# A decoder layer in which the low halves of the RWKV weights and the log decays move from GpSimd to VectorE

## The chip, the core and the metric

The kernel runs on one core of a Trainium2 chip. A core has five engines that run their own instruction queues in order and wait for each other by semaphores: TensorE (PE; its weight loads are listed as PEld), VectorE (DVE), ScalarE (ACT), GpSimd (POOL) and SyncE (SP), which here only issues DMAs. The metric is the device time of one execution in microseconds (us), lower is better. About 0.2% (3.2 us) is what a measurement of this kernel can tell from no change.

## What is computed

One layer with two branches that share an input projection and an output projection; the norms and the attention are left out here.

```python
xn = rms_norm(h, norm_w)
p = jnp.einsum('bsd,dn->bsn', xn, w_in)            # 1024 x 1024 by 1024 x 8320, fp32
p_tm = p[..., :SHIFT_COLS]                          # r, k, v, decay rank, iclr rank
p_tm = p_tm + (prev - p_tm) * mu_shift              # token shift
y_rwkv = rwkv7_time_mix(p_tm, p[..., RWKV_GATE0:ATT0], ...)
y_att = mixed_dilated_attention(p[..., ATT0:ATT_GATE0], p[..., ATT_GATE0:])
h = h + jnp.einsum('bsm,md->bsd', jnp.concatenate([y_rwkv, y_att], -1), w_out)

# in rwkv7_time_mix, for 16 heads of 64:
w = -jax.nn.softplus(-(w0 + jnp.tanh(w_lo) @ w_up)) - 0.5
decay = jnp.exp(-jnp.exp(w))                        # log decay = -exp(-0.5) * sigmoid(...)
state = (state * w_t[:, :, None, :] + sa[..., None] * bv_t[:, :, None, :]
         + v_t[..., None] * k_t[:, :, None, :])     # one step of the recurrence
```

## The kernel before

**Projections.** A product of fp32 precision is made of three products of fp32r parts: x is split into a high part `xh` and a low part `xl`, and each block of 128 columns of `w_in` into `wh` and `wl`. `wload` (L169) brings one such block in two halves of 128 x 512 (`wraw`, two buffers), ScalarE rounds a half to `wh` (L178), and GpSimd subtracts it from the raw half to make `wl` (L179). `wh` and `wl` have two buffers each, so a block can be split as soon as TensorE has done the last product with the block before the last. `stream` (L190) is a generator that loads one block ahead and yields after each of the 24 products of a block and a half of the tokens (`pq`, L187).

**The RWKV stage.** There are 16 units: 8 pairs of heads times 2 halves of 512 tokens; unit n is half n mod 2 of pair n // 2, so odd units are second halves. A unit runs a chain of 8 chunks of 64 tokens, each of three steps (`chain`, L636): `z` from the state (`Sd`), copied to `zd` by VectorE and ScalarE (L654, L655); `z` from `zd` and the inverse `U`, scaled to `ud` (L657, L658); and `T` from `ud` and `TU`, scaled to the next `Sd` (L657, L658). TensorE must wait for both halves of each copy. While one unit's chain runs, the next unit's matrices are prepared, those of the one after are begun, and the finished one is normed. `rwkv` (L287) puts all this into 24 slots a unit and fills TensorE with four projections a slot, 96 a unit.

**Decays.** In `prepare`, `decay` (L400) computes `th` by ScalarE (L408); GpSimd makes the log decays `lw` (L413) in a tile that shares its memory with `W`, after a memset of its last column (L412); VectorE sums them backwards in four scans (`I`, L422), and ScalarE's exponentials of `I` (`W`, `Ux`) scale `AR` and `BK`, from which TensorE makes `pa` (L527). VectorE masks one half of `pa` into `TU` (L530), ScalarE copies the other into `MV` (L533), and GpSimd masks that (L534).

**Order.** The order on an engine is not that of the code. A scheduler places every instruction when, by its own estimate of durations, its inputs are ready, and prefers what stands earlier in the code. A change of engine in one line thus moves other instructions too, on all engines.

After the RWKV stage come the attention, which takes its projections from the same stream (columns from `ATT0` on), and the output projection.

Of the kernel before, what the change touches and what calls it, by code (L numbers as in the profile page):

```python
# [9 lines left out]
F32 = mybir.dt.float32  # L10
# [3 lines left out]
ALU = mybir.AluOpType  # L14
# [10 lines left out]
C = 64  # L25
NC_ = HALF // C
LO0 = 3072
GATE0 = 3200
ATT0 = 4224
# [15 lines left out]
DECAY = float(np.exp(-0.5))  # L45
# [4 lines left out]
def bc(ap, shape):  # L50
    return ap.broadcast_to(list(shape))


class Kern:
# [111 lines left out]
                V.tensor_tensor(out=self.xl[h][:, 4 * b:4 * b + 4, ts], in0=q, in1=hi.bitcast(F32), op=ALU.subtract)  # L166
                yield

    def wload(self, src, wp):  # L169

        nc = self.nc
        wl = wp.tile([128, KT, 128], F32R, name="wl")
        wh = wp.tile([128, KT, 128], F32R, name="wh")
        for i in range(2):
            raw = wp.tile([128, KT // 2, 128], F32, name="wraw")
            ks = slice(4 * i, 4 * i + 4)
            nc.sync.dma_start(out=raw, in_=src[i * 512:(i + 1) * 512].rearrange("(kt p) c -> p kt c", p=128))
            nc.scalar.copy(out=wh[:, ks], in_=raw)  # L178
            nc.gpsimd.tensor_tensor(out=wl[:, ks], in0=raw, in1=wh[:, ks].bitcast(F32), op=ALU.subtract)  # L179
        return wh, wl  # L180

    def proj_steps(self, w, h, q):
# [6 lines left out]

    def stream(self, jobs):  # L190

        load = lambda job: self.wload(self.t["w_in"][:, job[0]:job[0] + 128], self.wp)
        w = load(jobs[0])
        for i, (_, halves, take) in enumerate(jobs):
            wn = load(jobs[i + 1]) if i + 1 < len(jobs) else None
            for h in halves:
                q = self.ps_proj.tile([128, HALF], F32, name="pq", tag="proj")
                steps = self.proj_steps(w, h, q)
                for m in steps[:-1]:
                    m()  # L200
                    yield
                steps[-1]()
                take(h, q)
                yield
            w = wn
# [85 lines left out]
    def rwkv(self, pairs=range(NPAIR), apairs=range(NPAIR)):  # L291
        nc = self.nc
        with ExitStack() as ctx:
# [21 lines left out]
            for a in self.ARs:  # L315
                nc.gpsimd.memset(a[:, NC_ * 192:], 0.0)
                a = self.c192(a)
                for e in range(2):
                    er = slice(e * 64, e * 64 + 64)
                    nc.gpsimd.tensor_copy(out=a[er, :, 0], in_=bc(self.ident[er, er].unsqueeze(1), (64, NC_, 64)))  # L320
            self.d0 = pers.tile([128, 2, C + 1], F32, name="d0")
            nc.gpsimd.memset(self.d0, 1.0)
            nc.gpsimd.memset(self.d0[:, :, C:C + 1], 0.0)
            bank = lambda p, tag: lambda: p.tile([128, 4, 128], F32, name="xq", tag=tag)
# [66 lines left out]
    def prepare(self, d):  # L391

        nc = self.nc
        V, S, G = nc.vector, nc.scalar, nc.gpsimd
        h, pr = d["h"], d["pr"]
        col = lambda base: self.prm[:, base + pr:base + pr + 1]
        c3 = lambda ap: ap.rearrange("p (c t) -> p c t", t=C)
        L = (128, NC_, C + 1)

        def decay():  # L400
            zq = self.ps_a.tile([128, HALF], F32, name="zq", tag="pa0")
            aq = self.ps_a.tile([128, HALF], F32, name="aq", tag="pa1")
            hi, lo = d["lw"]
            for i, q in enumerate((zq, aq)):
                nc.tensor.matmul(q, lhsT=hi[i], rhs=self.lx[h][i], start=True, stop=False)
                nc.tensor.matmul(q, lhsT=lo[i], rhs=self.lx[h][i], start=False, stop=True)
            th = self.tmp("gt0", "th")
            S.activation(out=th, in_=zq, func=AF.Tanh, scale=0.5, bias=self.hw0[:, pr:pr + 1])  # L408
            ta = d["ta"] = self.tmp("gt1", "ta")
            S.activation(out=ta, in_=aq, func=AF.Tanh, scale=0.5, bias=self.ha0[:, pr:pr + 1])  # L410
            lw = self.tmp("vr0", "lw", L)
            G.memset(lw[:, :, C:C + 1], 0.0)  # L412
            G.tensor_scalar(out=lw[:, :, 0:C], in0=c3(th), scalar1=-DECAY / 2, scalar2=-DECAY / 2,  # L413
                            op0=ALU.mult, op1=ALU.add)
            d["lw_"], d["I"] = lw, self.tmp("gt0", "I", L)

        def sums(i):

            for c in (4 * i, 4 * i + 2):
                fl = lambda a, c=c: a[:, c:c + 2].rearrange("p c t -> p (c t)")[:, ::-1]  # L420
                z0 = fl(self.d0, 0)
                V.tensor_tensor_scan(out=fl(d["I"]), data0=z0, data1=fl(d["lw_"]), initial=0.0, op0=ALU.mult,  # L422
                                     op1=ALU.add)
            if i == 0:
                return
            I = d["I"]
            W = d["W"] = self.tmp("vr0", "W", L)
            S.activation(out=W, in_=I, func=AF.Exp, scale=-1.0)
            Ux = d["Ux"] = self.tmp("vr1", "Ux", L)
            S.activation(out=Ux, in_=I, func=AF.Exp)  # L430
            d["dec"] = self.mid.tile([64, 2, NC_], F32, name="dec", bufs=3)
            G.tensor_copy(out=d["dec"][:, 0], in_=Ux[0:64, :, 0])
            S.copy(out=d["dec"][:, 1], in_=Ux[64:128, :, 0])

        def norm():
            sq = self.tmp("qr1", "sq")
            S.activation(out=sq, in_=d["ks"], func=AF.Square, scale=col(P_KK))
            sqt = self.ps_tr.tile([128, 4, 2, HD], F32, name="sqt", tag="tr")
            for b in range(4):
                nc.tensor.transpose(out=sqt[:, b].rearrange("p a b -> p (a b)"), in_=sq[:, b * 128:(b + 1) * 128],  # L440
                                    identity=self.ident)
            nq = self.mid.tile([128, 4, 2], F32, name="nq")
            V.tensor_reduce(out=nq, in_=sqt, axis=AX.X, op=ALU.add)
            rn = d["rn"] = self.mid.tile([128, NC_], F32, name="rn", bufs=3)
            for par in range(2):
                for e in range(2):
                    V.tensor_scalar(out=rn[e * 64:e * 64 + 64, par::2], in0=nq[par * 64:par * 64 + 64, :, e], scalar1=1e-24,
                                    scalar2=-2.0, op0=ALU.max, op1=ALU.mult)
            V.reciprocal(out=rn, in_=rn)
            d["rn1"] = self.mid.tile([64, NC_], F32, name="rn1", bufs=3)  # L450
            S.copy(out=d["rn1"], in_=rn[64:128])

        def removal():
            ks, ta, W, Ux = d["ks"], d["ta"], d["W"], d["Ux"]
            BK = d["BK"] = self.lng.tile([128, NC_, 128], F32, name="BK", bufs=1)
            V.scalar_tensor_tensor(out=self.c192(d["AR"])[:, :, 2], in0=c3(ks), scalar=col(P_KK), in1=W[:, :, 0:C],
                                   op0=ALU.mult, op1=ALU.mult)
            b2 = BK[:, :, 0:64]
            V.scalar_tensor_tensor(out=b2, in0=c3(ta), scalar=1.0, in1=Ux[:, :, 1:C + 1], op0=ALU.add, op1=ALU.mult)
            V.scalar_tensor_tensor(out=b2, in0=c3(ks), scalar=col(P_KK), in1=b2, op0=ALU.mult, op1=ALU.mult)  # L460
            S.activation(out=ta, in_=ta, func=AF.Identity, scale=self.hka[:, pr:pr + 1], bias=self.oka[:, pr:pr + 1])
            V.tensor_tensor(out=ks, in0=ks, in1=ta, op=ALU.mult)
            V.tensor_tensor(out=BK[:, :, 64:128], in0=c3(ks), in1=Ux[:, :, 1:C + 1], op=ALU.mult)

        def receptance():
            V.tensor_tensor(out=self.c192(d["AR"])[:, :, 1], in0=c3(d["rs"]), in1=d["W"][:, :, 1:C + 1], op=ALU.mult)

        def bonus_parts():
            rs = d["rs"]
            V.scalar_tensor_tensor(out=rs, in0=rs, scalar=self.hrk[:, pr:pr + 1], in1=d["ks"], op0=ALU.mult, op1=ALU.mult)  # L470
            bh, bl = d["bs"] = [self.tmp(t, n, dt=F32R) for t, n in (("kr3", "bh"), ("vr3", "bl"))]
            S.copy(out=bh, in_=rs)
            G.tensor_tensor(out=bl, in0=rs, in1=bh.bitcast(F32), op=ALU.subtract)
        return list(zip(PREP, (norm, decay, lambda: sums(0), lambda: sums(1), removal, receptance, bonus_parts)))

    def late(self, d):
# [623 lines left out]
```

## Time and profile before

| | us |
|---|---|
| median of 3 runs (1586.15 to 1588.06) | 1586.47 |
| the profiled execution | 1586.58 |
| its span, from the first to the last instruction | 1584.9 |
| PE busy | 1492.5 |
| DVE busy | 1014.7 |
| ACT busy | 892.7 |
| POOL busy | 532.9 |

The span and the execution's time differ by 1.7 us, which lie outside the instructions. The profile is read here in four views: the page's sums and its chain of work that ended last; stretches of time with the busy time of each engine; the timeline, with each instruction's start and duration and the idle time of its engine before it; and groups of instructions by line. The busy time of TensorE is not its time at the peak, since its products overlap in the pipeline: what shows a stall is the distance from one start to the next.

### The profile page before, as it was taken

To read this page: it belongs to the slowest core of one execution; us is meant where nothing else is said; L and a number is where in the kernel's file an instruction comes from. 1 tells how busy PE (TensorE), PEld (TensorE's weight loads), DVE (VectorE), ACT (ScalarE), POOL (GpSimd) and SP (SyncE) were. 2 spreads that over 40 slices of the span, in tenths; PEclk is the share of its full clock that TensorE was granted. 3 is DMA by queue.
4 is the path that set the end of the run, shared out by engine and by line. 5 is a ranking of instruction groups with operands and counts; after the bars stand their busy time and mean duration, and the time that the engine had idled before them with its cause. 6 is when DMAs were issued, how large, how long until landed. Compare 5 with 4: busy or idle time off the path is not lost.

```text
span 1584.9 us, 29112 instructions
## 1 busy us (share of the span) xinstructions
PE 1492.5 (94%) x10721; PEld 1211.0 (76%) x10721; DVE 1014.7 (64%) x2686; ACT 892.7 (56%) x2080; POOL 532.9 (34%) x668
## 2 busy tenths in 40 slices
PE   5889999999999999999999999999999999999997
PEld 4677777777777777777677788888888888787886
DVE  5866767677666676666743557676675766856234
ACT  5546666666656666566654456556565555645231
POOL 5443132222222221232211433443333334355542
PEclk9999999999999999999999999999999999999999
DMA  6121111111111111111111201111111111436452
GB/s 195 56 67 38 34 40 42 35 45 28 39 45 33 46 39 26 47 31 45 31 40 35 68 28 34 39 50 34 34 34 41 47 48 47 157 103 193 134 166 99
DMA packets 178829, 94.87 MB, mean 60 GB/s; under 512 B 58413, under 2 KB 164606, under 8 KB 178686
## 3 DMA queue, kind: packets, MB, share of 16 engines
q1 hardware_dynamic: 174942, 86.19, 19.6%
q10 hardware_dynamic: 3744, 6.82, 1.3%
q8 instruction: 84, 1.38, 0.4%
q14 instruction: 59, 0.48, 0.1%
HBM read 75.01 MB, written 17.83 MB: 59 GB/s over the span
## 4 chain that ended last, share of the span: by engine, by line
PE 66%; DVE 18%; ACT 9%; issue 4%; POOL 1%; DMA 1%; DVEq 0%; SPq 0%; ACTq 0%; POOLq 0%
PE pq L187 31%; PE oq L984 10%; PE T L643 4%; PE z L643 3%; PE o L930 3%; PE pa L527 2%; PE mp L857 2%; PE sp L890 2%; DVE I L422 1%; PE sp L910 1%; PE sp L909 1%; ACT zt L724 1%; DVE TB L568 1%; ACT ud L658 1%; DVE UB L570 1%
## 5 line engine op out<-in xcount | busy, mean ns | idle before, releaser
L187 PE MATMUL pq<-xh,wh 128*128 128x512 f32 x1040 | 430.6, 414 | 0.0
L187 PE MATMUL pq<-xl,wh 128*128 128x512 f32 x1040 | 414.7, 399 | 0.0
L187 PE MATMUL pq<-xh,wl 128*128 128x512 f32 x1040 | 291.8, 404 | 0.0
L179 POOL TENSOR_TENSOR wl<-wraw,wh 128x512 fp32r<-128x512 f32 x138 | 181.1, 1328 | 173.9 <-issue 46.3
L187 PEld LDWEIGHTS pq<-xh,wh 128*128 128x128 f32 x1040 | 197.0, 190 | 32.6 <-issue 0.2
L187 PEld LDWEIGHTS pq<-xl,wh 128*128 128x128 f32 x1040 | 197.4, 190 | 31.2 <-DVE xl L166 0.2
L187 PEld LDWEIGHTS pq<-xh,wl 128*128 128x128 f32 x1040 | 187.8, 190 | 33.0
L918 POOL TENSOR_TENSOR pl<-p,ph 128x512 fp32r<-128x512 f32 (+2 forms) x96 | 102.0, 1068 | 202.7 <-ACT ph L917 182.4
L984 PE MATMUL oq<-ow,qr 128*128 128x512 f32 x512 | 162.2, 395 | 1.2 <-ACT ow L965 0.6
L859 DVE CUSTOM_DVE_ANT_0 mp<-mp,maskq 128x512 f32<-128x512 f32 (+1 forms) x192 | 105.5, 570 | 68.0 <-PE mp L857 59.5
L913 ACT ACTIVATE p<-p 128x512 f32<-128x512 f32 (+2 forms) x144 | 64.6, 452 | 103.8 <-DVE p L912 103.0
L979 POOL TENSOR_TENSOR vr<-kr,qr 128x512 fp32r<-128x512 f32 (+2 forms) x68 | 90.4, 1335 | 80.9 <-ACT qr L978 74.0
L984 PEld LDWEIGHTS oq<-ow,qr 128*128 128x128 f32 x512 | 95.9, 188 | 23.0 <-ACT ow L965 1.0
L984 PE MATMUL oq<-ow,vr 128*128 128x512 f32 x256 | 101.2, 395 | 1.9 <-POOL vr L979 1.9
L178 ACT CAST wh<-wraw 128x512 fp32r<-128x512 f32 x138 | 79.7, 618 | 40.6 <-PE pq L187 30.9
L978 ACT CAST qr<-kr 128x512 fp32r<-128x512 f32 (+2 forms) x68 | 40.2, 594 | 94.3 <-PE oq L984 53.1
L912 DVE TENSOR_TENSOR p<-sp,maskt 128x512 f32<-128x512 f32 (+2 forms) x144 | 65.3, 457 | 42.9 <-PE sp L910 41.4
L643 PEld LDWEIGHTS T<-ud,TU 128*128 128x128 f32 x256 | 39.6, 188 | 56.2 <-ACT ud L658 51.8
L643 PE MATMUL T<-ud,TU 128*128 128x128 f32 x256 | 59.4, 314 | 22.7 <-ACT ud L658 22.1
L657 DVE TENSOR_SCALAR Sd<-T,dec 64x64 f32<-64x64 f32 x120 | 33.0, 275 | 66.8 <-PE T L643 65.0
L658 ACT ACTIVATE ud<-z,rn 64x64 f32<-64x64 f32 x128 | 39.4, 308 | 56.5 <-DVE ud L657 54.9
L658 ACT ACTIVATE Sd<-T,dec 64x64 f32<-64x64 f32 x120 | 36.9, 308 | 57.0 <-DVE Sd L657 55.6
(235 smaller groups left out, 3126.6 us busy)
## 6 DMA issues: line engine op xcount, KB each, us to landing
wraw<-in_w_in_dram SPq DMA_DIRECT2D x138, 256.0 KB, 3.0
kr<-mixd SPq DMA_DIRECT2D x60, 256.0 KB, 3.0
oraw<-in_w_out_dram SPq DMA_DIRECT2D x16, 512.0 KB, 5.2
xt<-in_x_dram SPq DMA_DIRECT2D x8, 512.0 KB, 3.8
ld<-TU SPq DMA_DIRECT2D x32, 128.0 KB, 2.7
mixd<-zt SPq DMA_DIRECT2D x16, 256.0 KB
mixd<-gt SPq DMA_DIRECT2D x16, 256.0 KB, 2.2
xr<-in_x_dram ACTq DMA_DIRECT2D x16, 256.0 KB, 2.8
```

The lines of the kernel that those rows point to most:

```text
L178: nc.scalar.copy(out=wh[:, ks], in_=raw)
L179: nc.gpsimd.tensor_tensor(out=wl[:, ks], in0=raw, in1=wh[:, ks].bitcast(F32), op=ALU.subtract)
L187: return [lambda i=i, a=a, b=b: self.nc.tensor.matmul(q, lhsT=a, rhs=b, start=(i == 0), stop=(i == len(ops) - 1)) for i, (a, b) in enumera ...
L643: mm = lambda out, w, x, start, stop: nc.tensor.matmul(out, lhsT=w, rhs=f2(x), start=start, stop=stop, skip_group_check=True)
L658: S.activation(out=out[er[1], 1], in_=q[0:64, 64:128], func=AF.Copy, scale=scale[1])
L859: V.tensor_tensor_reduce(out=mp[:, :kn], in0=mp[:, :kn], in1=self.maskq[:, v0:v0 + kn], op0=ALU.add, op1=ALU.max, scale=1.0, scalar=-3e38, ...
L912: V.tensor_tensor(out=p[:, :qn], in0=sp[:, :qn], in1=self.maskt[:, u0:u0 + qn], op=ALU.add)
L913: S.activation(out=p[:, :qn], in_=p[:, :qn], func=AF.Exp)
L918: G.tensor_tensor(out=pl[:, :qn], in0=p[:, :qn], in1=ph[:, :qn].bitcast(F32), op=ALU.subtract)
L930: nc.tensor.matmul(oc, lhsT=v, rhs=w[:, :qn], start=(first and i == 0), stop=(last and i == len(prods) - 1), skip_group_check=True)
L979: nc.gpsimd.tensor_tensor(out=ml, in0=raw, in1=mh.bitcast(F32), op=ALU.subtract)
L984: nc.tensor.matmul(q, lhsT=m[:, i], rhs=v, start=(k == 0 and j == 0), stop=(k == 15 and j == 2))
```

## The change

Two things move from GpSimd to VectorE: the subtraction that makes `wl`, for the projections of the RWKV branch alone (columns below `ATT0`, 37 blocks, 74 halves; the attention's blocks keep GpSimd), and the log decays `lw`. `lw` gets a tile of its own, cleared once, so the memset of each unit is gone.

```diff
-    def wload(self, src, wp):
+    def wload(self, src, wp, eng):
...
             nc.scalar.copy(out=wh[:, ks], in_=raw)
-            nc.gpsimd.tensor_tensor(out=wl[:, ks], in0=raw, in1=wh[:, ks].bitcast(F32), op=ALU.subtract)
+            eng.tensor_tensor(out=wl[:, ks], in0=raw, in1=wh[:, ks].bitcast(F32), op=ALU.subtract)
...
-        load = lambda job: self.wload(self.t["w_in"][:, job[0]:job[0] + 128], self.wp)
+        load = lambda job: self.wload(self.t["w_in"][:, job[0]:job[0] + 128], self.wp,
+                                      self.nc.vector if job[0] < ATT0 else self.nc.gpsimd)
...
             self.d0 = pers.tile([128, 2, C + 1], F32, name="d0")
+            self.lw = pers.tile([128, NC_, C + 1], F32, name="lw")
+            nc.gpsimd.memset(self.lw, 0.0)
...
-            lw = self.tmp("vr0", "lw", L)
-            G.memset(lw[:, :, C:C + 1], 0.0)
-            G.tensor_scalar(out=lw[:, :, 0:C], in0=c3(th), scalar1=-DECAY / 2, scalar2=-DECAY / 2,
+            lw = self.lw
+            V.tensor_scalar(out=lw[:, :, 0:C], in0=c3(th), scalar1=-DECAY / 2, scalar2=-DECAY / 2,
                             op0=ALU.mult, op1=ALU.add)
```

Lines behind the edits are numbered one to three higher in the changed kernel (L223 becomes L224, L654 becomes L656). The order of the instructions changes on every engine of the RWKV stage; from the attention on it is the same. Three places show it.

The first is VectorE at the start of the chain of an odd unit (unit 3), around the first copy of `z` to `zd`. `TB` and `UB` are the columns of the next unit's inverse, `vs` is the shifted projection, `gs` belongs to the norm of the unit before. Before:

```order
L657 TENSOR_SCALAR Sd_122<-T_2736,dec 64x64
L570 TENSOR_TENSOR UB<-UB,TB 64x11x5
L568 TENSOR_TENSOR TB<-UB,AB 64x48
L570 TENSOR_TENSOR UB<-UB,TB 64x12x4
L568 TENSOR_TENSOR TB<-UB,AB 64x39
L570 TENSOR_TENSOR UB<-UB,TB 64x13x3
L654 COPY zd_126<-z 64x64
L223 SCALAR_TENSOR_TENSOR vs_3002<-pq,om,shtmp 128x512
L705 TENSOR_REDUCE gs<-Y 128x8
```

And after:

```order
L659 TENSOR_SCALAR Sd_122<-T_2728,dec 64x64
L570 TENSOR_TENSOR TB<-UB,AB 64x39
L179 TENSOR_TENSOR wl<-wraw,wh 128x512 x2
L224 SCALAR_TENSOR_TENSOR vs_2994<-pq,om,shtmp 128x512
L656 COPY zd_126<-z 64x64
L707 TENSOR_REDUCE gs<-Y 128x8
```

Both halves of a block's `wl` and the shift `vs` now stand ahead of the copy `zd`. The even units have one half ahead of `zd`, and the shift and the other half behind it.

The second is TensorE at the same place: the projections between the transposes `tq` and the product that needs `zd`. Before:

```order
L496 MATMUL tq<-ident,BK 128x128 x4
L187 MATMUL pq<-xh_78,wh 128x512
L187 MATMUL pq<-xl_80,wh 128x512
L187 MATMUL pq<-xh_78,wh 128x512
L187 MATMUL pq<-xl_80,wh 128x512
L643 MATMUL z<-zd_126,U_119 66x128
```

And after:

```order
L498 MATMUL tq<-ident,BK 128x128 x4
L187 MATMUL pq<-xh_78,wh 128x512
L187 MATMUL pq<-xl_80,wh 128x512
L187 MATMUL pq<-xh_78,wh 128x512
L187 MATMUL pq<-xl_80,wh 128x512
L187 MATMUL pq<-xh_78,wh 128x512
L187 MATMUL pq<-xl_80,wh 128x512
L187 MATMUL pq<-xh_78,wh 128x512
L645 MATMUL z<-zd_126,U_119 66x128
L187 MATMUL pq<-xl_80,wh 128x512
L442 MATMUL sqt<-ident,sq 128x128 x4
```

Seven projections stand ahead of the product with `zd` where four did, and the transposes `sqt` have moved ahead of the next product with `ud`.

The third is VectorE in the middle of a unit (unit 4), where the second block of the unit is split. `TU` is the masked half of `pa`, `LT` and `UT` are transposes for the next unit's inverse. Before:

```order
L470 SCALAR_TENSOR_TENSOR rs<-rs,hk,ks 128x512
L586 STREAM_TRANSPOSE LT<-TU 128x512
L530 TENSOR_TENSOR TU<-pa_3867,mask 64x4x128
L530 TENSOR_TENSOR TU<-pa_3866,mask 64x4x128
L657 TENSOR_SCALAR Sd_122<-T_3599,dec 64x64
L530 TENSOR_TENSOR TU<-pa_3918,mask 64x4x128
L654 COPY zd_126<-z 64x64
L223 SCALAR_TENSOR_TENSOR rs_3904<-pq,om,shtmp 128x512
L530 TENSOR_TENSOR TU<-pa_3917,mask 64x4x128
L657 TENSOR_SCALAR ud_128<-z,rn 64x64
```

And after:

```order
L588 STREAM_TRANSPOSE LT<-TU 128x512
L593 STREAM_TRANSPOSE UT<-U_119 128x512
L532 TENSOR_TENSOR TU<-pa_3855,mask 64x4x128
L532 TENSOR_TENSOR TU<-pa_3854,mask 64x4x128
L659 TENSOR_SCALAR Sd_122<-T_3589,dec 64x64
L179 TENSOR_TENSOR wl<-wraw,wh 128x512
L224 SCALAR_TENSOR_TENSOR rs_3892<-pq,om,shtmp 128x512
L532 TENSOR_TENSOR TU<-pa_3906,mask 64x4x128
L656 COPY zd_126<-z 64x64
L179 TENSOR_TENSOR wl<-wraw,wh 128x512
L532 TENSOR_TENSOR TU<-pa_3905,mask 64x4x128
L659 TENSOR_SCALAR ud_128<-z,rn 64x64
```

One half of `wl` and the shift `rs` stand ahead of `zd`, the other half ahead of `ud`; the transpose `UT` has come down from an earlier place in the unit.

## Rows read from the trace of the kernel before

**Rows 1.** The page: busy time of each engine; the chain that ended last.

```profile
PE 1492.5 (94%) x10721; PEld 1211.0 (76%) x10721; DVE 1014.7 (64%) x2686; ACT 892.7 (56%) x2080; POOL 532.9 (34%) x668
...
PE 66%; DVE 18%; ACT 9%; issue 4%; POOL 1%; DMA 1%; DVEq 0%; SPq 0%; ACTq 0%; POOLq 0%
```

**Rows 2.** Stretches: start:end, length, busy us of each engine, granted clock, DMA.

```profile
128.00:762.00 634.00, 594.91 (x5757) 467.54 (x5755) 436.97 (x1334) 393.89 (x1030) 165.64 (x288) 1.00 0.16 38
...
884.00:1585.00 701.00, 683.58 (x3317) 574.14 (x3315) 428.64 (x952) 365.88 (x739) 292.86 (x260) 0.99 0.25 76
```

**Rows 3.** Instructions of L179 before 745 us, and of L413: ns min/median/max.

```profile
L179 POOL TENSOR_TENSOR wl<-wraw,wh x74: 1259/1282/1753, 12.9 to 738.1; 128x512 fp32r<-128x512 f32 x74
...
L413 POOL TENSOR_SCALAR lw<-th x16: 615/622/622, 58.3 to 768.7; 128x512 f32<-128x512 f32 x16
```

**Rows 4.** Timeline, start of unit 3: start, duration, instruction, [idle before <-releaser].

```profile
272.18 2.52 POOL L179 TENSOR_TENSOR wl<-wraw,wh 128x512 fp32r<-128x512 f32 x2 [1.85 <-issue]
...
272.27 1.23 DVE L570 TENSOR_TENSOR UB<-UB,TB 64x48 f32<-64x48 f32 x1
...
273.54 1.20 DVE L568 TENSOR_TENSOR TB<-UB,AB 64x39 f32<-64x39 f32 x1
273.67 0.40 PE L187 MATMUL pq<-xh,wh 128*128 128x512 f32 x1
273.91 0.39 PE L187 MATMUL pq<-xl,wh 128*128 128x512 f32 x1
274.78 0.19 DVE L570 TENSOR_TENSOR UB<-UB,TB 64x39 f32<-64x39 f32 x1
274.89 0.21 DVE L654 COPY zd<-z 64x64 f32<-64x64 f32 x1
...
275.39 0.43 PE L643 MATMUL z<-zd,U 128*66 128x128 f32 x2 [1.09 <-ACT zd L655]
...
277.25 0.49 PE L643 MATMUL T<-ud,TU 128*128 128x128 f32 x2 [0.50 <-ACT ud L658]
```

**Rows 5.** Timeline, VectorE at the starts of unit 1 and of unit 13.

```profile
174.45 1.24 DVE L568 TENSOR_TENSOR TB<-UB,AB 64x28 f32<-64x28 f32 x1
...
758.91 1.24 DVE L568 TENSOR_TENSOR TB<-UB,AB 64x28 f32<-64x28 f32 x1
```

**Rows 6.** Timeline, start of unit 4, and the copy that starts unit 5.

```profile
321.39 2.53 POOL L179 TENSOR_TENSOR wl<-wraw,wh 128x512 fp32r<-128x512 f32 x2 [1.85 <-issue]
...
323.20 0.79 DVE L706 TENSOR_SCALAR gs<-gs 128x8 f32<-128x8 f32 x1
...
325.81 0.38 PE L643 MATMUL T<-ud,TU 128*128 128x128 f32 x1 [0.71 <-ACT ud L658]
...
372.95 0.20 DVE L654 COPY zd<-z 64x64 f32<-64x64 f32 x1
```

**Rows 7.** Timeline, middle of unit 4.

```profile
334.18 0.75 DVE L422 TENSOR_TENSOR_SCAN I<-d,lw 128x130 f32<-128x130 f32 x2 [1.86 <-POOL lw L413]
...
348.23 0.68 DVE L530 TENSOR_TENSOR TU<-pa,mask 64x512 f32<-64x512 f32 x1 [0.95 <-PE pa L527]
...
348.35 0.67 POOL L534 TENSOR_SCALAR_AFFINE_SELECT MV<-MV 64x512 f32<-64x512 f32 x1
...
350.15 0.75 DVE L223 SCALAR_TENSOR_TENSOR rs<-pq,om,shtmp 128x512 f32<-128x512 f32 x1 [0.99 <-ACT shtmp L220]
```

**Rows 8.** Groups on VectorE: line, shapes, count, busy us, mean ns, idle before.

```profile
L657 DVE TENSOR_SCALAR Sd<-T,dec 64x64 f32<-64x64 f32 x120 | 33.0, 275 | 66.8 <-PE T L643 65.0
...
L539 DVE TENSOR_TENSOR TU<-TU,rn 128x512 f32<-128x512 f32 x16 | 12.7, 794 | 0.1
...
L462 DVE TENSOR_TENSOR ks<-ks,ta 128x512 f32<-128x512 f32 x16 | 11.1, 692 | 5.0 <-ACT ta L461 4.8
```

**Rows 9.** Timeline of the first 70 us: VectorE and TensorE.

```profile
14.39 2.49 DVE L68 TENSOR_SCALAR rs_w<-rs_x 128x2 int32<-128x2 int32 x1
...
66.65 1.64 DVE L463 TENSOR_TENSOR BK<-ks,Ux 128x512 f32<-128x512 f32 x1
...
68.44 1.59 PE L527 MATMUL pa<-AR,BK 64*128 64x128 f32 x16 [3.92 <-DVE BK L463]
```

## What I expect of the change, before it was run

> **What bounds the kernel now.** I read the page first, then stretches of time, then the timeline at the places where the order changes, and last the groups by line. TensorE is busy for 1492.5 of 1584.9 us, and the chain that ended last is 66% TensorE and 18% VectorE, with POOL at 1% [rows 1]. So POOL, from which the change takes work, sets almost nothing by itself; VectorE, which gets it, is second on the chain. The change can only act in the RWKV stage: from the attention on, the 701 us from 884 to 1585 [rows 2], the order is the same. In the middle of the stage, 128 to 762 us, TensorE is busy for 594.9 of 634 us and VectorE for 437 [rows 2]; the 39 us left on TensorE, and what its pipeline hides beside them, are all that can be won there. The granted clock is 1.00 there, so clock is no issue.
>
> What TensorE waits for is the chain of a unit. At the start of unit 3 the product with `zd` waits 1.09 us and the one with `ud` 0.50 [rows 4]. In front of that `zd` stand two small subtractions on VectorE that take 1.23 and 1.20 us, while the next of nearly the same size takes 0.19 [rows 4]. They lie inside the 2.52 us of POOL's two halves of `wl`, from 272.18 to 274.70, and time returns to normal at its end: VectorE's operations with two inputs in SBUF are held while POOL's subtraction runs. The same 1.24 us stands at the start of unit 1 and of unit 13 [rows 5], so it comes seven times, in units 1, 3, ... 13. At the start of unit 4 the halves end when a small `gs` operation takes 0.79 in place of some 0.2, and the product with `ud` waits 0.71 [rows 6]. So POOL does not appear on the chain but makes VectorE long there, and that is what the change can take away. From the copy of unit 3 to that of unit 5, 274.89 to 372.95, two units take 98.06 us [rows 4, 6].
>
> **The change, part by part.** It removes from POOL 74 halves of 1.28 us and 16 log decays of 0.62 us [rows 3]. VectorE has no subtraction into a rounded type in these groups; the nearest row by shape and by inputs is `ks` with 0.692 us, two inputs of 128x512 [rows 8], and I take 0.69 a half. For `lw` (one input, 128x512) the rows bound it by 0.275 (same kind, 64x64) and 0.692 (same size, two inputs) [rows 8]; near neither, so the middle, 0.48. A steady unit has four halves, two at its start and two in its middle.
>
> *Starts of odd units, 7 times.* From the first held operation to `zd` pass 274.89 - 272.27 = 2.62 us before. After, one small operation (0.19), two halves (1.38) and the shift (0.75, as the `rs` of the same line takes [rows 7]) stand there: 2.32. So `zd` comes 0.3 earlier, if the halves find `wh` ready. Besides, seven projections instead of four stand on TensorE before the product with `zd`; three more at the 0.24 us from one start to the next (273.67 to 273.91) fill 0.7 of the 1.09 wait, and the transposes `sqt` now fill the 0.50 before `ud` [rows 4]. What fills a wait is taken from another place, where it may leave a hole; with nothing known of that I count half of the 1.2. That gives -0.3 - 0.6 = -0.9 (range -0.3, none of the filling, to -1.5, all of it): 7 x -0.9 = -6.3 us.
>
> *Starts of even units, 6 times.* The hold of 0.6 goes, one half of 0.69 comes ahead of `zd`: +0.1. The other half and a reduction come ahead of `ud`, for which TensorE already waits 0.71 [rows 6], so that what is late on VectorE is late on TensorE: between nothing and +0.69, half of it taken. Sum +0.4 (range -0.6, hold gone and halves hidden, to +0.8): 6 x +0.4 = +2.4 us. Queued behind the halves here are `zd` and `ud` themselves, and TensorE's chain behind them.
>
> *Middles, 13 times.* In the middle of unit 4 VectorE idles for 0.95 us before a `TU` and 0.99 before the shift [rows 7], 1.94 in all; the two halves, 1.38, come about there, before `zd` and before `ud`. I cost them at nothing, under this cover; without it they cost 1.38. With POOL's halves goes what they add to the mean of `TU` scaled by `rn`, 0.794 against 0.692 for the like shape [rows 8], -0.1. The scans wait 1.86 us for `lw` [rows 7], of which POOL's own operation is 0.62; on VectorE it is 0.48, so -0.14, range -0.35 to +0.07. The rest of that wait is for `th`, and stays. The memset is off the path. Against it, POOL's select of `MV` takes 0.67 right beside VectorE's work there [rows 7], and as POOL holds VectorE at the unit starts, so it may hold a half that now stands there: up to +0.67. Sum -0.24 (range -0.45 to +0.74): 13 x -0.24 = -3.1 us.
>
> *Before the first unit.* In the first 70 us two holds are on the path: the start of the norm, an operation on 128x2 that takes 2.49 us instead of some 0.2, and `BK`, 1.64 against 0.69, for which TensorE waits 3.92 [rows 8, 9]. Together 2.3 + 0.95 = 3.25 go. Halves on VectorE come in their place, two of them assumed, 1.38: -1.9 us (range -3.3, halves hidden, to +1.4, holds not on the path).
>
> The sum is -6.3 + 2.4 - 3.1 - 1.9 = -8.9 us on the profiled execution, 1586.58, which is 0.1 above the median of the runs: 1577.7, **1578 us**. With all terms at their good ends, -10.5 - 3.6 - 5.9 - 3.3 = -23.3, 1563; all at the bad ends, -2.1 + 4.8 + 9.6 + 1.4 = +13.7, 1600.
>
> VectorE's busy time says how much room is left: in 128 to 762 us it gets 13 x (4 x 0.69 + 0.48) = 42 us and loses 7 x 2 + 6 x 0.6 = 18 of holds, 437 to about 461 of 634, 73%. It stays below TensorE's, and 120 of its `Sd` copies wait 65 us in all for TensorE's `T` [rows 8], half a microsecond each: mostly VectorE is ahead at that point of the chain.
>
> **The rivals.**
>
> *VectorE is held in its turn (slower).* The place is the middle of a unit. The halves move to the engine, but POOL keeps the selects, each 0.67 us and reading SBUF [rows 7]; they need what TensorE and ScalarE make at the very time at which the halves are placed. If both halves are held for a whole select, they take 1.36 each, 2.72 against the idle 1.94: +0.78 a unit, 13 x 0.78 = +10.1. At the odd starts other POOL work would eat the 0.3 and leave a shorter filling, 0; the even starts +0.6 x 6 = +3.6; before the first unit -1.9. Sum +11.8, about **1598**. The point from which it decides is a mean half over 0.97 us on VectorE, where two no longer fit into 1.94. For it: the 0.794 of `TU` shows that VectorE loses time to POOL in mid-unit [rows 8]. Against it: that row contains holds by 1.28 us long halves too, which go, and a select of 0.67 beside 0.68 of `TU` in row 348.35 and 348.23 shows one side running undisturbed, though that `TU` reads PSUM [rows 7].
>
> The Trainium skill (SBUF — State Buffer, section "SBUF: two separate sides") has this as a rule: VectorE with two inputs in SBUF and a GpSimd operation that reads SBUF take an exclusive lock on shared ports, and the second waits for the whole instruction of the first. The 1.23 and 1.20 us next to 0.19 agree [rows 4]. By it the move doesn't end the collisions but makes them shorter, since the halves on VectorE are of the kind that takes the lock; that is this rival.
>
> *The lead is given back (same).* What VectorE wins at the odd starts is lost at the next wait: the shift and the norm's chain come later on it at the even starts, and the projections that fill the odd starts are missing elsewhere. Then odd -0.3 x 7 = -2.1, even +2.4, middles 0, before -1.9: -1.6, **1585**. For it: TensorE waits behind the same chain at each step, and 48 copies a unit pass through VectorE and ScalarE; against it: the 0.7 of filling is at places where TensorE surely idled.
>
> *All holds go and all halves are hidden (faster still).* The good ends above, **1563**. For it: 31% of VectorE's time is idle in the stage. Against it: the idle time is not where the halves stand at the even starts.
>
> **How the numbers follow.** The forecast, 1578 with its own terms varying between 1568 and 1583, gets 0.60, for the holds are seen in rows and their removal is sure. The rival of the lock gets 0.17, the lead given back 0.16, the good ends 0.07. From no change a measurement of this kernel can tell 0.2%, 3.2 us, so faster is 0.60 + 0.07 = 0.67, same 0.16, slower 0.17. The range goes from 1563, the good end, to 1593, which leaves out the worse part of the lock's rival, about 0.12, and what lies below, 0.05.
>
> **What would show it.** In the profile of the changed kernel the 74 halves on VectorE should have a mean of 0.69 to 0.75 us; over 0.97 the lock's rival holds. At the odd starts no small subtraction takes over 0.5 us, and the product with `zd` waits 0.6 or less instead of 1.09. At the even starts the product with `ud` waits about 1 us instead of 0.71. Two units should take some 97.2 us instead of 98.06 (-0.9 + 0.4 - 0.48). VectorE is busy for about 461 us in the same units, and the 701 us of the attention and the output stay within 1 us. I am wrong if the halves in VectorE's queue wait for ScalarE's `wh` with `z` already there, or if TensorE starts to wait for the third product's `wl`.

## The result, and the profile after

The changed kernel takes 1562.1 us (median of four runs, 1560.75 to 1567.6) against 1587.3 beside it, 0.9849 of the time (95% interval 0.9824 to 0.9873): 24 us faster. The forecast was 1578 and the low end of the range 1563, just above the measured time. The direction was right, the size nearly three times too small: 8.9 us were forecast. The profiled execution has a span of 1560.8 us against 1584.9.

First the page, as in [rows 1]: busy time of each engine, and the chain that ended last.

```profile
PE 1490.8 (96%) x10721; PEld 1211.8 (78%) x10721; DVE 1029.8 (66%) x2776; ACT 891.8 (57%) x2080; POOL 455.3 (29%) x563
...
PE 67%; DVE 18%; ACT 10%; issue 3%; DMA 1%; POOL 1%; DVEq 0%; SPq 0%; POOLq 0%; ACTq 0%
```

VectorE got 15.1 us more to do in all and POOL 77.6 less. The moved halves and log decays, by line (count, busy us and mean ns; for the log decays ns min/median/max):

```profile
L179 DVE TENSOR_TENSOR wl<-wraw,wh 128x512 fp32r<-128x512 f32 x74 | 51.5, 708 | 13.1 <-ACT wh L178 6.8 <-PE pq L187 5.1
...
L415 DVE TENSOR_SCALAR lw<-th x16: 411/427/430, 54.8 to 745.2; 128x512 f32<-128x512 f32 x16
```

A half takes 0.708 us (0.69 was taken), a log decay 0.43 (0.48 was taken, between bounds of 0.275 and 0.692). The Trainium skill (VectorE: DVE Perf Modes, section "The perf-mode tier table") puts `tensor_scalar` on fp32 in SBUF at twice the base speed and `tensor_tensor` at the base speed. The 0.427 beside 0.708 for the same shape agrees in direction; the factor between the whole instructions is 1.66 here.

The stretches of [rows 2] (start:end, length, busy us of each engine, clock, DMA), the second shifted by the 24 us:

```profile
128.00:762.00 634.00, 609.60 (x5924) 481.52 (x5926) 465.67 (x1441) 405.15 (x1060) 118.17 (x215) 1.00 0.15 39
...
860.00:1561.00 701.00, 683.14 (x3315) 573.77 (x3313) 428.81 (x952) 365.36 (x739) 293.59 (x260) 0.99 0.25 76
```

The last 701 us are unchanged (TensorE busy for 683.14 us against 683.58), as was expected. To see where the 24 us arise, one instruction is followed: the first copy `zd` of a unit. It starts 9.1 us earlier in unit 0 (128.31 before, 119.18 after), 14.4 in unit 3 (274.89 in [rows 4], 260.45 here), 24.5 in unit 11, and 24.4 in unit 14. VectorE's timeline, before (unit 11, unit 14):

```profile
663.91 0.21 DVE L654 COPY zd<-z 64x64 f32<-64x64 f32 x1
...
802.82 0.21 DVE L654 COPY zd<-z 64x64 f32<-64x64 f32 x1
```

and after:

```profile
639.45 0.20 DVE L656 COPY zd<-z 64x64 f32<-64x64 f32 x1
...
778.41 0.22 DVE L656 COPY zd<-z 64x64 f32<-64x64 f32 x1 [1.27 <-PE z L645]
```

So there are four parts: 9.1 us before the first chain; 5.3 in units 0 to 2; from unit 3 to unit 11 another 10.0 in eight units, 1.25 a unit; and at unit 13 the lead is at 26.9 (761.99 to 735.05) and falls to 24.4 a unit later. Each figure is of one execution. Experiments (9) to (12) below edit later blocks alone, and in their traces the first copy starts 7.9 to 9.3 us earlier than before; so the first part is known to about one us.

The start of unit 3, which answers to [rows 4], on VectorE and TensorE (start, duration, idle before and its releaser):

```profile
258.06 0.28 DVE L659 TENSOR_SCALAR Sd<-T,dec 64x64 f32<-64x64 f32 x1
258.26 0.18 DVE L570 TENSOR_TENSOR TB<-UB,AB 64x39 f32<-64x39 f32 x1
258.58 1.29 DVE L179 TENSOR_TENSOR wl<-wraw,wh 128x512 fp32r<-128x512 f32 x2
259.79 0.74 DVE L224 SCALAR_TENSOR_TENSOR vs<-pq,om,shtmp 128x512 f32<-128x512 f32 x1
260.45 0.21 DVE L656 COPY zd<-z 64x64 f32<-64x64 f32 x1
...
261.97 0.43 PE L645 MATMUL z<-zd,U 128*66 128x128 f32 x2 [0.52 <-ACT zd L657]
```

The operations of 1.2 us are gone, the wait for `zd` fell from 1.09 to 0.52 and that for `ud` from 0.50 to nothing. What is left of the first is no longer VectorE's: its `zd` is done at 260.66, ScalarE's half starts only at 261.72, behind four copies of transposes.

The start of unit 4, which answers to [rows 6]:

```profile
306.11 0.69 DVE L179 TENSOR_TENSOR wl<-wraw,wh 128x512 fp32r<-128x512 f32 x1
306.72 0.21 DVE L656 COPY zd<-z 64x64 f32<-64x64 f32 x1
...
307.82 0.68 DVE L179 TENSOR_TENSOR wl<-wraw,wh 128x512 fp32r<-128x512 f32 x1
308.43 0.68 DVE L707 TENSOR_REDUCE gs<-Y 128x8 f32<-128x512 f32 x1
309.02 0.27 DVE L659 TENSOR_SCALAR ud<-z,rn 64x64 f32<-64x64 f32 x1
...
309.68 0.49 PE L645 MATMUL T<-ud,TU 128*128 128x128 f32 x2 [0.16 <-ACT ud L660]
```

Here a loss was forecast, and the wait for `ud` fell from 0.71 to 0.16. At the other even units from 2 to 12 it was 0.69 or 0.70 and is 0.15, 0.16 or nothing.

### The profile page after: what moved, and what is told of

Read it like the earlier page. It is cut to its first block, busy times and chain, and to the rows that moved or that the text cites. A ratio compares the mean times of both kernels' runs of the same rounds, so it can differ in the third digit from the quotient of the medians.

```text
span 1560.8 us, 29095 instructions
## 1 busy us (share of the span) xinstructions
PE 1490.8 (96%) x10721; PEld 1211.8 (78%) x10721; DVE 1029.8 (66%) x2776; ACT 891.8 (57%) x2080; POOL 455.3 (29%) x563
## 4 chain that ended last, share of the span: by engine, by line
PE 67%; DVE 18%; ACT 10%; issue 3%; DMA 1%; POOL 1%; DVEq 0%; SPq 0%; POOLq 0%; ACTq 0%
PE pq L187 33%; PE oq L986 10%; PE T L645 4%; PE z L645 3%; PE o L932 3%; PE mp L859 2%; PE sp L892 2%; PE pa L529 2%; PE sp L912 1%; PE sp L911 1%; ACT zt L726 1%; DVE wl L179 1%; ACT MV L535 1%; PE x L621 1%; DVE I L424 1%
## 5 line engine op out<-in xcount | busy, mean ns | idle before, releaser
L179 POOL TENSOR_TENSOR wl<-wraw,wh 128x512 fp32r<-128x512 f32 x64 | 85.2, 1351 | 110.5 <-ACT Sd L660 36.2
```

Of the source, the lines that this page charges most:

```text
L179: eng.tensor_tensor(out=wl[:, ks], in0=raw, in1=wh[:, ks].bitcast(F32), op=ALU.subtract)
```

## The experiments

All are the kernel before or the changed one with one thing different. Times are medians, ratios are against the kernel before on the same chip.

**Are the parts additive? (1) The low halves alone.** `lw` is made as before, by POOL in its shared tile with its memset.

```diff
-            lw = self.lw
-            V.tensor_scalar(out=lw[:, :, 0:C], ...)
+            lw = self.tmp("vr0", "lw", L)
+            G.memset(lw[:, :, C:C + 1], 0.0)
+            G.tensor_scalar(out=lw[:, :, 0:C], ...)
```

> Only the low halves go to VectorE; the log decays and their memset stay on POOL as before. Theory H (the gain is VectorE no longer held by POOL's long subtractions): nearly the whole gain, 1562 to 1566 us. Rival L (the log decays carry a good part, since the scans wait 1.86 us for them in the middle of a unit): 1570 to 1580.

1567.0 us, ratio 0.9875 (0.986 to 0.989): the larger part of the gain, some 4 us short of all. The interval touches that of the changed kernel (0.9824 to 0.9873); (3) separates the two.

**(2) The log decays alone.**

```diff
-                                      self.nc.vector if job[0] < ATT0 else self.nc.gpsimd)
+                                      self.nc.gpsimd)
```

> Only the log decays go to VectorE; the low halves stay on POOL. Theory H: the holds stay, 1584 to 1588 us, no change that can be measured. Rival L: 1570 to 1580. Rival O (the new order of the instructions makes the gain, whatever engine the halves run on): this order is nearer to that of before on VectorE and nearer to the changed kernel's on TensorE, so some 1575.

1586.0 us, ratio 1.0001 (0.9992 to 1.0011): nothing. So the log decays are worth nothing alone and some 4 us on top of the halves.

**(3) The new tile alone.** The changed kernel with `G.tensor_scalar` in place of `V.tensor_scalar`.

> The changed kernel, with the log decays on POOL again but in their own tile, cleared once. The kernel with the low halves alone (log decays on POOL, in the tile that they share with W) gave 1567 us, 5 more than the changed one. If the own tile is what helps (no memset, no wait for W to be read), 1561 to 1563; if VectorE's making of them helps, 1566 to 1568.

1567.4 us, ratio 0.9884 (0.9871 to 0.9898), as (1), and 5 us above the changed kernel. It is the engine, not the tile. With the log decays on POOL the group of the scans on VectorE (busy us, mean ns, idle us before) reads:

```profile
L424 DVE TENSOR_TENSOR_SCAN I<-d,lw 128x130 f32<-128x130 f32 x64 | 25.2, 416 | 26.0 <-POOL lw L415 26.0
```

in the changed kernel:

```profile
L424 DVE TENSOR_TENSOR_SCAN I<-d,lw 128x130 f32<-128x130 f32 x64 | 23.8, 410 | 0.5
```

In the changed kernel 16.1 us of waiting for `th` stand before `lw` itself instead; 9.4 are saved of the 26.0, 0.6 us for each of the 16.

**POOL holds, or the order of the instructions? (4) POOL repeats the subtraction.** VectorE's result is used; POOL does the work again, into the raw half.

```diff
             eng.tensor_tensor(out=wl[:, ks], in0=raw, in1=wh[:, ks].bitcast(F32), op=ALU.subtract)
+            # for the 74 halves:
+            nc.gpsimd.tensor_tensor(out=raw, in0=raw, in1=wh[:, ks].bitcast(F32), op=ALU.subtract)
```

> The changed kernel, in which POOL repeats each of the 74 subtractions behind VectorE's, into the raw half that nobody reads any more (work added, the output stays the same). The order on TensorE is that of the changed kernel for 7996 of 8051 rows. Theory H: POOL's collisions with VectorE return at full length, 1580 to 1595 us, with operations of 1.2 us and more on VectorE at the unit starts again. Rival O (order): 1562 to 1566, since POOL's queue has room and nobody waits for what it writes but the next load of the half.

1576.4 us, ratio 0.9943 (0.992 to 0.9965): 14 of the 24 us are lost again, less than theory H said and more than O. By the copies `zd`, 7.0 of them are lost before the first chain (the lead there is 2.1 instead of 9.1) and 7.4 in units 0 to 11 (it grows by 9.9 instead of 17.3). **(5) POOL writes zeros instead**, nearly as long (two memsets of 0.525 us against 1.29) and, like it, right behind VectorE's half, but without reading: `nc.gpsimd.memset(raw, 0.0)`, twice.

> As e5_pool_again, but POOL writes zeros twice into the raw half (some 0.53 us each by the rows of a memset of this size) instead of the subtraction: POOL is as busy and as late, but reads nothing from SBUF (work added, the output stays the same). Theory H in its strict form (it is POOL's reading that holds VectorE): 1561 to 1566 us. Rival Q (POOL's queue is what costs, its masks and small operations come later): 1572 to 1578, as e5_pool_again with 1576.

1562.1 us, ratio 0.9849 (0.9832 to 0.9865): nothing is lost. POOL's queue is not the cause; its reading is.

The order on VectorE is not quite the same in the two, so the time alone doesn't settle it; the rows do. `TB` and `UB` are 480 small operations with two inputs in SBUF. In the kernel before, 19 of them take over 0.5 us, 22.1 us together; in the changed kernel 3; in (4) 12, with 13.2 us; in (5) the two at the start of unit 13, which stand beside a subtraction that POOL still makes there (see (10)). The two traces side by side at the start of unit 3. With the repeated subtraction, POOL and VectorE:

```profile
269.02 2.90 POOL L179 TENSOR_TENSOR wraw<-wraw,wh 128x512 f32<-128x512 f32 x2 [2.58 <-DVE wl L179]
...
269.45 0.75 DVE L224 SCALAR_TENSOR_TENSOR vs<-pq,om,shtmp 128x512 f32<-128x512 f32 x1
270.12 0.20 DVE L656 COPY zd<-z 64x64 f32<-64x64 f32 x1
270.25 0.67 DVE L707 TENSOR_REDUCE gs<-Y 128x8 f32<-128x512 f32 x1
270.84 1.14 DVE L572 TENSOR_TENSOR UB<-UB,TB 64x39 f32<-64x39 f32 x1
```

and with the memsets:

```profile
257.32 1.57 POOL L179 MEMSET wraw<- 128x512 f32 x3 [2.55 <-DVE wl L179]
...
258.44 0.21 DVE L656 COPY zd<-z 64x64 f32<-64x64 f32 x1
258.57 0.19 DVE L570 TENSOR_TENSOR TB<-UB,AB 64x48 f32<-64x48 f32 x1
258.69 0.67 DVE L707 TENSOR_REDUCE gs<-Y 128x8 f32<-128x512 f32 x1
```

During POOL's subtraction the shift and the copy, which read PSUM, and the reduction, which has one input, keep their usual time, while `UB`, with two inputs in SBUF, is held until POOL is done, 1.14 us instead of 0.18. During the memsets the like `TB` takes 0.19. In (4) the hold falls behind `zd`, where it costs little: TensorE waits 0.55 there, 0.52 in the changed kernel. That, the smaller number of holds, and an order on TensorE which is nearly the changed kernel's are the likely reasons why (4) keeps 10 of the 24 us although POOL does as much as before. How much of these 10 is the place of the holds and how much the order itself isn't separated.

**What does VectorE's time cost? (6) VectorE subtracts twice**, the second time into the raw half.

```diff
+            # for the 74 halves:
+            nc.vector.tensor_tensor(out=raw, in0=raw, in1=wh[:, ks].bitcast(F32), op=ALU.subtract)
```

> The changed kernel, in which VectorE makes each of the 74 subtractions twice, the second time into the raw half that nobody reads any more (work added, 74 x 0.69 = 51 us on VectorE, the output stays the same). It asks what VectorE's time costs. If VectorE has room (73% busy in the stage), 1563 to 1573 us; if VectorE's time is on the path at every unit, a good part of the 51 us, 1585 to 1613.

1577.0 us, ratio 0.9947 (0.9932 to 0.9962). The second copies take 50.9 us of VectorE and cost 15, 0.3 us for each us. It lies between the two expectations, so VectorE's time is neither free nor the bound. By the copies `zd` the price is uneven: in units 1 to 11 the lead grows by 1.2 us instead of 15.0, so 44 second copies, some 30 us, cost 13.8 there; what the others cost and gain nets to little. VectorE's order changes much in this run, so the price is that of time and order together.

**Where does the gain arise? (7) Only the first 11 blocks**, all before the first chain, on VectorE, and **(8) only those from the twelfth on**; `lw` as before in both.

```diff
-                                      self.nc.vector if job[0] < ATT0 else self.nc.gpsimd)
+                                      self.nc.vector if n < 11 else self.nc.gpsimd)
+                                      # (8): 11 <= n and job[0] < ATT0
```

> Only the first 11 blocks (22 halves, all before the chain of unit 0) are split by VectorE; the other blocks and the log decays stay on POOL. In the trace of the changed kernel the first copy of z comes 9.1 us earlier than before, while I had forecast 1.9. If this gain is the start's own and is kept, 1576 to 1579 us; if the later units give it back or it needs the log decays, 1582 to 1587.

> The opposite part of e3_first11: VectorE makes the low halves from the twelfth block on (52 halves), POOL those of the first 11 blocks and the log decays. If start and later units add up (18.5 us of the low halves alone, 5.6 of them at the start), 1572 to 1575 us; if the start's gain and that of the units share a cause (the order of the whole), 1566 to 1570 or 1578 to 1584.

(7) takes 1579.8 us, ratio 0.9957 (0.994 to 0.9973); (8) takes 1578.1, ratio 0.9951 (0.9936 to 0.9966). Both parts are real. By the ratios they give 6.8 and 7.8 us, 14.6 together, against 19.8 for (1), with intervals of some 2.5 us each. The copies `zd` show where the two fall short: not in units 0 to 11, where the lead grows by 12.6 us in (8) and 12.5 in (1), but before the first chain (6.0 us in (7) and -0.6 in (8), against 7.6) and in unit 13 (1.9 lost in (8), 0.9 in (1)).

**(9) The middles of the units.** POOL keeps the 26 halves that are split in the middle of a unit (every second block from the twelfth on).

```diff
+                                      self.nc.vector if job[0] < ATT0 and (n < 11 or n % 2) else self.nc.gpsimd)
```

> The changed kernel, in which POOL keeps the halves that are split in the middle of a unit (every second block from the twelfth on, 13 blocks, 26 halves); VectorE makes those before unit 0 and at the unit starts, and the log decays. I had forecast 0.1 us a unit from taking POOL's halves out of the middle. If only the starts gain, 1560 to 1564; if VectorE's time in the middle is on the path (e6_dve_twice: 15 us for 51 us), 13 x 2 x 0.69 x 0.29 = 5 us less, 1556 to 1560; if POOL's halves in the middle hold VectorE on the path as well, 1566 to 1572.

1562.7 us, ratio 0.986 (0.9839 to 0.9881): as the changed kernel. In the middle it makes no difference that can be measured which engine makes the halves.

**The loss in unit 13. (10) The first block of the attention on VectorE too**, `n < 38` in the selection.

> The changed kernel, with the first block of the attention (two more halves) on VectorE too. In the changed kernel the two halves of that block run on POOL at 732.39 us and hold two small subtractions of VectorE for 1.24 and 1.20 us at the start of unit 13; TensorE then waits 1.50, and the granted clock is 0.77 in the 5 us behind. In unit 13 the lead over the kernel before falls from 26.9 to 23.8 us. If the hold and the clock after it are its cause, 3 us come back: 1558 to 1560 us against 1562. If the end of the stage loses them whatever POOL does, 1561 to 1563.

1558.8 us, ratio 0.9829 (0.9814 to 0.9844): 3 us less by the medians, with an interval that overlaps the changed kernel's. The trace shows the place: in unit 13 the lead rises by 3.0 us, to 29.6, where in the changed kernel it falls by 2.5. In the changed kernel POOL splits this block and holds VectorE at the start of unit 13, as it did before at each odd unit. POOL, VectorE, TensorE:

```profile
732.39 2.50 POOL L179 TENSOR_TENSOR wl<-wraw,wh 128x512 fp32r<-128x512 f32 x2 [1.85 <-issue]
...
732.46 1.24 DVE L570 TENSOR_TENSOR TB<-UB,AB 64x28 f32<-64x28 f32 x1
733.73 1.20 DVE L572 TENSOR_TENSOR UB<-UB,TB 64x28 f32<-64x28 f32 x1
...
735.55 0.43 PE L645 MATMUL z<-zd,U 128*66 128x128 f32 x2 [1.50 <-ACT zd L657]
```

In this execution TensorE's granted clock then falls, from its upper level of 2.4 GHz to a mean of 0.77 of it. The five us behind, in the changed kernel:

```profile
735.00:740.00 5.00, 4.05 (x17) 3.06 (x18) 3.97 (x11) 2.91 (x8) 0.42 (x2) 0.77 0.41 114
```

and with the block on VectorE:

```profile
735.00:740.00 5.00, 4.47 (x26) 3.39 (x24) 4.32 (x14) 3.58 (x10) 0.00 (x0) 1.00 0.35 105
```

The fall of the clock is not a fixed part of the hold. In (4), (5) and (9) POOL holds VectorE there too and TensorE waits 1.52 to 1.54 us, but the clock stays at 1.00 in the ten us behind; the lead then falls by 1.4 to 1.5 us in place of 2.5.

**(11) All blocks loaded during the stage** (`n < 43`), and **(12) all 138 halves** on VectorE.

> The changed kernel, with the first six blocks of the attention on VectorE, that is, all that are loaded while the RWKV stage still runs. e7_att1 with one of them gave 1558.8 us. If POOL's other halves at the starts of units 14 and 15 hold VectorE on the path too, 1556 to 1558; if only the first one stood in front of a copy that TensorE waits for, 1558 to 1560; if VectorE's time costs more there, 1560 to 1563.

> All 138 halves on VectorE, in the attention too, where VectorE is busy for 429 of 701 us. Theory H: POOL's subtractions hold VectorE there as well, so a further gain, 1552 to 1558 us. Rival: e6_dve_twice showed that 51 us more on VectorE cost 15 us in the RWKV stage; 64 halves x 0.69 = 44 us at the same price are 13 us, of which little is won back: 1562 to 1572.

(11) takes 1556.3 us, ratio 0.9813 (0.98 to 0.9827); (12) takes 1556.1, ratio 0.9818 (0.9805 to 0.9831). Both lie 0.003 to 0.004 below the changed kernel's ratio, about the least that the intervals can tell; from each other and from (10) they don't separate them. In the attention the engine of the halves makes no difference that can be measured.

## Why the prediction was right or wrong, point by point

**The mechanism was right.** POOL's reading subtraction holds VectorE's two-input operations; (4) against (5) shows that reading is what does it, and (1) and (2) that the halves carry the gain. The rival by which the collisions go on at VectorE's expense (1598) fell: the mean half is 0.708 us, far below the 0.97 from which it would decide. That the halves collide now and then shows in single rows, 1.67 us for one at 66.34 beside a subtraction of POOL for `bl` from 66.11 to 67.46, not in the mean. The measured time is that of the rival with all terms at their good ends (1563), but it isn't made up as that rival said: of its terms only the even starts came out at their good end, the odd starts near the middle of their range, and the start far beyond its own. That the time falls so near to 1563 is luck.

**Before the first unit: the largest miss.** -1.9 was forecast (range to -3.3), 9.1 us were won in the trace, and (7) shows 6.8 end to end for the halves alone. The step that failed is the choice of rows: two holds in the first 70 us were counted [rows 9], and the stretch from 70 to 128 us was left out of the sum. There POOL holds VectorE once more, before:

```profile
92.40 2.56 POOL L179 TENSOR_TENSOR wl<-wraw,wh 128x512 fp32r<-128x512 f32 x2 [5.47 <-ACT wh L178]
...
92.28 0.22 DVE L570 TENSOR_TENSOR UB<-UB,TB 64x64 f32<-64x64 f32 x1
92.53 1.25 DVE L568 TENSOR_TENSOR TB<-UB,AB 64x63 f32<-64x63 f32 x1
93.81 1.22 DVE L570 TENSOR_TENSOR UB<-UB,TB 64x63 f32<-64x63 f32 x1
...
104.71 2.08 PE L527 MATMUL pa<-AR,BK 64*128 64x128 f32 x16 [4.21 <-DVE BK L463]
```

The two small operations lose some 2 us, and VectorE is busy with hardly a gap from there to the `BK` for which TensorE waits 4.21. The like product after:

```profile
95.06 1.16 PE L529 MATMUL pa<-AR,BK 64*128 64x128 f32 x16 [0.96 <-DVE UB L572]
```

Nor was the clock read there. [rows 2] shows it for the steady stretch alone, where it is 1.00. Behind the long waits of the start it was lower, before:

```profile
40.00:50.00 10.00, 7.35 (x33) 5.85 (x32) 8.91 (x15) 4.77 (x9) 2.46 (x5) 0.83 0.19 53
70.00:80.00 10.00, 9.73 (x46) 7.71 (x46) 7.40 (x10) 6.65 (x11) 5.84 (x7) 0.88 0.23 51
100.00:110.00 10.00, 5.79 (x30) 4.23 (x28) 7.79 (x13) 4.53 (x10) 3.08 (x7) 0.66 0.11 16
```

and after it was 1.00 in each of the three:

```profile
100.00:110.00 10.00, 9.42 (x49) 6.82 (x52) 5.63 (x11) 4.62 (x9) 2.38 (x5) 1.00 0.26 54
```

So in these traces a wait was paid twice, once as idle time and once as slower products (`pa` above takes 2.08 and 1.16 us). But part of this may be chance: in 70 to 80 us the clock was 0.66 in (7) and 0.83 in (10), which both start with VectorE's halves, and 1.00 in the changed kernel. How the 9.1 us divide between idle time and clock was not separated.

**Starts of odd units: right step, right size, one too many.** The forecast took `zd` 0.3 earlier and half of the filling, -0.9. In unit 3 the two idle times fell by 0.57 + 0.50 = 1.07 us; in units 5 and 9, which had no wait for `ud` before, by 0.7; the mean of units 1 to 11 is 1.0. These are six starts and not seven, for unit 13 kept its hold (below).

**Starts of even units: wrong sign.** +0.4 was forecast, as what is late on VectorE would be late on TensorE. The row itself says otherwise: the wait of 0.71 ended with ACT's `ud` [rows 6]. On ScalarE the square for the norm stood ahead of `ud`, before:

```profile
324.80 0.63 ACT L709 ACTIVATE ysq<-Y 128x512 f32<-128x512 f32 x1 [0.56 <-ACT MV L501]
325.45 0.31 ACT L658 ACTIVATE ud<-z,rn 64x64 f32<-64x64 f32 x1
```

after:

```profile
309.32 0.31 ACT L660 ACTIVATE ud<-z,rn 64x64 f32<-64x64 f32 x1 [0.45 <-DVE ud L659]
310.18 0.63 ACT L711 ACTIVATE ysq<-Y 128x512 f32<-128x512 f32 x1 [0.55 <-DVE Y L709]
```

The norm's chain now comes later on VectorE, behind the halves, and so its square comes behind `ud` on ScalarE. I named the later norm as a loss and looked at the order of VectorE and TensorE alone; the order of ScalarE, the releaser in the row, decided. Over units 2 to 12 the wait fell by 0.6 a start, 6 us from the forecast in all.

**Middles: the halves right, the log decays too small.** That the halves cost and gain nothing there, -0.1, is what (9) shows. The log decays were taken as -0.14 a unit, by the difference of two durations; (3) against the changed kernel gives 5 us over 16 units, 0.3 each, and the scans' waits fell by 0.6 each. The difference of two durations is thus not the whole price of a step that passes from one engine to another and back; what the rest consists of was not separated. Alone, without the halves, they bring nothing (2), which no term of the sum held.

**The end of the stage: not seen.** The section on the change says that the attention's blocks keep POOL, and the first of them is split at the start of unit 13, one of my seven odd starts [rows 5]. That hold thus stayed: 0.9 us were counted there, and the lead fell by 2.5 (10).

**The pace.** Two units were to take 97.2 us. From [rows 4, 6] and 355.21 for unit 5 it is 94.76 after against 98.06; but the pattern repeats only after four units, and over eight units (unit 3 to 11) a pair takes 97.26 before and 94.75 after: -2.5 where -0.9 was forecast (the three terms in the forecast's bracket add up to -0.98, so its 97.2 should have been 97.1). One pair was too short a sample. Of the 2.5, the rows above give 1.0 at the odd start, 0.6 at the even one and, by (3), 0.6 for the two log decays; the rest was not found. Busy VectorE came out as 465.7 for 461.

## What to carry to other kernels

Work on POOL that reads SBUF costs VectorE's time even where POOL is on no chain: look for operations of VectorE that take several times their usual duration, and check for each whether it stands ahead of something that TensorE waits for. Before costing a later instruction, read which engine the wait's releaser names, and follow the order on that engine. Read the whole span by stretches, the start and the hand-over between stages too, with the clock of each: the holds at the start were worth nearly as much as eight steady units. One trace's clock in such a stretch is a sample: read a second execution before you count on it.

## What the runs showed that I had not expected

- A memset on POOL does not hold an operation of two inputs in SBUF (`TB` 0.19 us within 1.57 us of memsets, (5)). But in the kernel before the operation on 128x2 with one input at 14.39 us [rows 9] ends at 16.88, with a memset that ends at 16.86, and not with the subtraction at 15.55. POOL's rows there:

```profile
14.29 1.26 POOL L179 TENSOR_TENSOR wl<-wraw,wh 128x512 fp32r<-128x512 f32 x1
...
15.82 0.52 POOL L573 MEMSET U<- 128x512 f32 x1
16.29 0.12 POOL L550 MEMSET UB<- 64x16 f32 x1
16.34 0.52 POOL L573 MEMSET U<- 128x512 f32 x1
```

POOL's instructions follow each other without a gap there, from 14.29 to 16.86. The Trainium skill (SBUF — State Buffer, section "SBUF: two separate sides") tells the two apart: two SBUF inputs collide only with a POOL operation that reads SBUF, a VectorE mode that uses two ports with any. Both rows agree, if the operation on 128x2 ran in such a mode, which no row shows.

- The price of VectorE's time, 15 us for 51 (6), beside a share of 73% busy in the stage: with three quarters of the time taken, 0.3 of each added us came through, and nearly half of it in units 1 to 11.
